# A hand-written order of all engines in the up projection of a convolutional feed-forward layer, with gated products on VectorE and sums of weights spread over the tiles

## The chip, the cores and the metric

The kernel runs on one core of a Trainium2 chip. Five engines run side by side, each with an instruction queue of its own, served in order, and they wait for each other with semaphores: TensorE (PE in the profile, its weight loads PEld), VectorE (DVE), ScalarE (ACT), GpSimd (POOL) and SyncE (SP), which here issues the transfers. The metric is the device time of one execution in microseconds, as the median of several runs. The result must agree with the reference in float32; matrix products therefore work with operands that are split in two.

## The reference

One transformer-like layer over 512 tokens of width 1024: a mixer of a state-space branch and a sparse attention, a feed-forward layer with a short convolution, and a gated embedding. The part that the change touches is the feed-forward layer:

```python
h = h + conv_ffn(rmsnorm(h, g_ffn[i]), w_up[i], conv_w[i], conv_b[i], w_down[i])

def conv_ffn(x, w_up, conv_w, conv_b, w_down):
    hid = x @ w_up                                   # 512 x 1024 @ 1024 x 5632
    hid = lax.conv_general_dilated(hid, conv_w[:, None, :], window_strides=(1,), padding=[(CONV_WIDTH - 1, 0)], ...) + conv_b
    a, b = jnp.split(hid, 2, axis=-1)
    return (jax.nn.gelu(a) * b) @ w_down             # 2816 x 1024
```

## The kernel before

**Split products.** Each float32 operand is held as a high part (ScalarE's `copy` into fp32r, L75) and a low part (the difference, `tt(lo, src, hi, SUB)`, L54). A product is three matmuls (`mm3`, L82 to L84): high by high, high by low, low by high. For the up projection these are `wh` with `n2h`, `wh` with `n2l` and `wl` with `n2h`, where `n2h` and `n2l` are the normalized activations.

**Tiles of the up projection.** The hidden width 2816 is cut in NF = 22 tiles of 128. Tile f has an a half (PSUM tile `ua`) and a b half (`ub`), each with a 1024 x 128 block of `w_up`, that is 8 blocks of contraction with 3 matmuls of 128 x 512 each: 48 matmuls for a tile. `wload` loads a raw block into one of three buffers `wr` (512 KB, L188), ScalarE copies the high part `wh`, and the low part `wl` is made by VectorE for the a half and by GpSimd for the b half; `wh` and `wl` have two buffers each. Tiles 0 and 1 are done in pieces, together with the end of the stage before; from f = 2 on all tiles are alike.

**Convolution and gate.** `convolved` takes each half from PSUM: ScalarE writes `cv` with one weight and the bias (L1495), VectorE adds the two delayed terms (`stt`, L63, 128 x 511 and 128 x 510). Then ScalarE does the Gelu of the a half (L1499). `Summed.add` makes the gated product in two pieces of 128 x 256 on GpSimd and, for the down projection, splits it (`ffa`, on ScalarE and VectorE) and forms sums of the pieces (`ffs`: S1 to S4) on VectorE. The down projection multiplies matrices in 2 x 2 blocks with seven products in place of eight, which is what all those sums are for. A hidden tile with odd number (e = 1) has three more of these steps than an even one.

**Sums of weights.** For the same reason sums of blocks of `w_down` are needed (`park`: two loads of 512 KB into tiles `b`, four additions of 128 x 512 on VectorE), and sums of blocks of `w_ple_gate` (`gate_parks`: four loads into `gb`, five sums, each split into `gph` on ScalarE and `gpl` on VectorE). They are made inside the up projection and written to DRAM (`bs`, `gs`) by `store_sums` and `leave`, and are loaded again later. `park_at` says at which tile each of the eleven blocks of `w_down` is done: two at f = 2, one at f = 3 and 8, one at each of 13 to 19. The gate sums lie at f = 2 to 12.

**What sets the order.** In the up projection no order is written out: a scheduler orders every engine's instructions by estimated times, with hints (`tc.issue_after(last(engine))`) that place the work on the sums of weights behind what its engine was given last. From the down projection on, TensorE, SP, ScalarE and VectorE run as written (`tc.manual_schedule`).

## Time and profile before

| | us |
|---|---|
| median of 3 runs | 791.77 (791.34 to 793.2) |
| the profiled execution | 793.93 |
| its span in the trace | 792.2 |
| TensorE / VectorE / ScalarE / GpSimd busy | 769.6 / 613.9 / 433.3 / 270.5 |
| up projection, f = 2 to 21 | 406.73 to 632.41 in the span |

The page of the profile gives busy times, and then the groups of instructions by line. A row of a timeline has the start, the duration, the engine, the line of the code, the operation, the tile written and the tiles read, and the size; in square brackets stands the idle time before it and what ended it. A row of waits has the waiting engine, tile and line, what it waited for, the sum of the waits, their number and the longest. Matmuls overlap in the pipeline, so the distance between two starts is the cost of one, not its duration.

### The profile page before, as it was taken

What the parts mean: (1) busy time and instruction counts of PE and PEld (TensorE: products, weight loads), DVE (VectorE), ACT (ScalarE), POOL (GpSimd) and SP (SyncE); (2) the same over time, 40 slices, a digit from 0 to 9 for tenths busy, and PEclk for the clock granted to TensorE, in tenths of its full rate; (3) what the DMA queues carried; (4) which work ended last, traced back from release to release, by engine and by line L of the source; (5) the groups of instructions that cost most, each with busy time, mean ns of one, the idle gap of its engine ahead of it and who ended that gap; (6) DMA issues with size and microseconds to landing.
All of it is one profiled execution on the core that took longest, in us unless ns stands there. A gap on an engine that the chain in (4) does not pass through costs nothing.

```text
span 792.2 us, 12336 instructions
## 1 busy us (share of the span) xinstructions
PE 769.6 (97%) x4362; PEld 645.7 (82%) x4362; DVE 613.9 (77%) x1152; ACT 433.3 (55%) x779; POOL 270.5 (34%) x303
## 2 busy tenths in 40 slices
PE   9999999999999999999999999999999999999993
PEld 7887878888888888888998887887777888888883
DVE  7987999766677739798696889987677587877586
ACT  6836655657777654435645454543434465745754
POOL 3577433136464534001125344432332310000125
PEclk9999999999999999999999999999999999999997
DMA  8944121424234136201097597567885365668752
GB/s 340 366 160 149 60 89 48 141 77 109 56 107 153 61 121 252 88 19 54 23 399 273 209 345 245 190 247 273 294 271 180 133 233 205 226 213 293 277 213 106
DMA packets 52077, 144.54 MB, mean 182 GB/s; under 512 B 6192, under 2 KB 8624, under 8 KB 52016
## 3 DMA queue, kind: packets, MB, share of 16 engines
q1 hardware_dynamic: 51440, 142.71, 51.5%
q10 hardware_dynamic: 576, 1.05, 0.4%
q8 instruction: 34, 0.56, 0.3%
q14 instruction: 27, 0.22, 0.1%
HBM read 112.28 MB, written 27.26 MB: 176 GB/s over the span
## 4 chain that ended last, share of the span: by engine, by line
PE 70%; DVE 15%; DMA 5%; issue 3%; POOL 3%; ACT 2%; SPq 1%; POOLq 0%; DVEq 0%; ACTq 0%
PE pj L82 6%; PE pj L83 5%; PE pj L84 5%; PE p L84 4%; PE p L82 4%; PE p L83 4%; DMA b<-in_w_down_dram 4%; DVE b L54 3%; DVE cv L63 2%; PE ua L84 2%; PE ua L83 2%; PE ua L82 2%; PE sps L1089 2%; PE ub L84 2%; PE ptp L1109 2%
## 5 line engine op out<-in xcount | busy, mean ns | idle before, releaser
L54 POOL TENSOR_TENSOR wl<-wr,wh 128x1024 fp32r<-128x1024 f32 x45 | 113.4, 2521 | 239.2 <-ACT wh L75 224.9
L75 ACT ACTIVATE wh<-wr 128x1024 fp32r<-128x1024 f32 x96 | 100.7, 1050 | 81.0 <-issue 24.5
L82 PE MATMUL pj<-n1h,wh 128*128 128x512 f32 x224 | 90.9, 406 | 0.4 <-DVE QT L54 0.4
L83 PE MATMUL pj<-n1l,wh 128*128 128x512 f32 x224 | 87.9, 392 | 0.0
L84 PE MATMUL pj<-n1h,wl 128*128 128x512 f32 x224 | 87.7, 392 | 0.0
L54 DVE TENSOR_TENSOR wl<-wr,wh 128x1024 fp32r<-128x1024 f32 (+1 forms) x51 | 64.3, 1261 | 22.5 <-ACT wh L75 21.8
L84 PE MATMUL ub<-n2h,wl 128*128 128x512 f32 (+1 forms) x168 | 65.3, 389 | 2.9 <-POOL wl L54 2.9
L84 PE MATMUL ua<-n2h,wl 128*128 128x512 f32 (+1 forms) x168 | 64.7, 385 | 1.5 <-DVE wl L54 1.5
L82 PE MATMUL ua<-n2h,wh 128*128 128x512 f32 (+1 forms) x168 | 64.8, 386 | 0.7 <-ACT wh L75 0.7
L83 PE MATMUL ua<-n2l,wh 128*128 128x512 f32 (+1 forms) x168 | 64.7, 385 | 0.0
L82 PE MATMUL ub<-n2h,wh 128*128 128x512 f32 (+1 forms) x168 | 64.6, 385 | 0.0
L83 PE MATMUL ub<-n2l,wh 128*128 128x512 f32 (+1 forms) x168 | 64.5, 384 | 0.0
L84 PEld LDWEIGHTS pj<-n1h,wl 128*128 128x128 f32 x224 | 42.1, 188 | 8.9
L82 PEld LDWEIGHTS pj<-n1h,wh 128*128 128x128 f32 x224 | 42.1, 188 | 8.4 <-DVE QT L54 0.9
L83 PEld LDWEIGHTS pj<-n1l,wh 128*128 128x128 f32 x224 | 42.2, 188 | 7.4 <-issue 0.2
L60 POOL TENSOR_SCALAR pr<-pr,su,gates 128x512 f32<-128x512 f32 (+2 forms) x64 | 38.7, 618 | 16.5 <-DVE su L1101 16.1
L54 POOL TENSOR_TENSOR cv<-cv 128x256 f32<-128x256 f32 x22 | 21.6, 983 | 61.1 <-DVE cv L63 47.2
L75 ACT ACTIVATE ph<-ptp 128x128 fp32r<-128x128 f32 (+1 forms) x64 | 27.9, 435 | 26.1 <-PE ptp L1109 26.0
L54 DVE TENSOR_TENSOR pl<-ptp,ph 128x128 fp32r<-128x128 f32 (+1 forms) x64 | 31.1, 486 | 14.3 <-ACT ph L75 13.3
L63 DVE SCALAR_TENSOR_TENSOR cv<-ub,cols,cv 128x511 f32<-128x511 f32 (+1 forms) x44 | 32.8, 744 | 12.0 <-ACT cv L1495 11.2
L84 PEld LDWEIGHTS ub<-n2h,wl 128*128 128x128 f32 x168 | 31.6, 188 | 11.5 <-POOL wl L54 5.5
L84 PEld LDWEIGHTS ua<-n2h,wl 128*128 128x128 f32 x168 | 31.6, 188 | 8.6 <-DVE wl L54 2.4
(509 smaller groups left out, 2108.8 us busy)
## 6 DMA issues: line engine op xcount, KB each, us to landing
wr<-in_w_up_dram SPq DMA_DIRECT2D x44, 512.0 KB, 4.6
wr<-in_w_in_dram SPq DMA_DIRECT2D x28, 512.0 KB, 3.9
b<-in_w_down_dram SPq DMA_DIRECT2D x22, 512.0 KB, 5.8
bs<-b SPq DMA_DIRECT2D x44, 256.0 KB, 2.5
ue<-bs SPq DMA_DIRECT2D x21, 512.0 KB, 4.5
wr<-in_w_down_dram SPq DMA_DIRECT2D x11, 512.0 KB, 4.9
gs<-gph SPq DMA_DIRECT2D x10, 512.0 KB, 2.6
gs<-gpl SPq DMA_DIRECT2D x10, 512.0 KB, 3.2
```

The costliest lines, as they stand in the source:

```text
L54: e.tensor_tensor(o, a, b, op=op)
L60: e.tensor_scalar(o, a, s1, s2, op0=op0, op1=op1)
L63: e.scalar_tensor_tensor(o, a, s, b, op0=op0, op1=op1)
L75: S.activation(o, a, AF.Copy)
L82: PE.matmul(ps, lh, rh, start=start, stop=False, skip_group_check=goes_on)
L83: PE.matmul(ps, lh, rl, start=False, stop=False, skip_group_check=goes_on)
L84: PE.matmul(ps, ll, rh, start=False, stop=stop, skip_group_check=goes_on)
L1089: PE.matmul(o, self.QQ[:, x, qt * P:(qt + 1) * P], KK[:, :, self.g, :w] if both else KK[:, self.br, self.g, :w], start=x == 0, stop=x == 1)
L1109: PE.transpose(ps[:, (qt - kt) * P:(qt - kt + 1) * P], self.pr[qt][:, kt * P:(kt + 1) * P], ident)
```

## The change

Nothing that is computed changes. From f = 2 on, all five queues are written out in one order of the program (`manual_schedule` over all engines):

- *TensorE.* In each half of a tile the 16 matmuls with `wh` come first (`up_half`), then the 8 with `wl` (`up_end`).
- *GpSimd* keeps the low part of the b half; the gated products (`times`) go to VectorE. Only the products of tiles 0 and 21 stay on GpSimd.
- *The gate of a tile is done one tile later*, with the convolution of its b half: `conv(f - 1, 1)` and `hidden(f - 1)` stand in tile f, `conv(f, 0)` and `gelu(f)` at its end. `Summed.add` is taken apart in `times`, `high`, `low` and `low2` for this.
- *Weights.* `up_high` and `up_low` make the parts of tile f + 1 at the end of tile f, apart from `up_low(f, 1, G)`, which stands in tile f.
- *Sums of weights* get new places (`down_at`, `half_at`, `gate_at`: the gate sums at f = 5 to 14; block 10 of `w_down` is done half at f = 8 and half at f = 12). Each is cut in a `first` part (`sums_a`) and a `second` part (`sums_z`, at the tile's end). Loads for `w_down` stand a tile ahead of their sums, and stores in the tile behind (`leave`), after that tile's loads.

```diff
-        def add(self, e, x, y):
-            tt(x[:, :HT], x[:, :HT], y[:, :HT], MUL, G)
-            tt(self.A22 if e else self.S1, x[:, HT:], y[:, HT:], MUL, G)
-            split(*self.A[e], x[:, :HT])
+        def times(self, e, x, y, v=V):
+            tt(x[:, :HT], x[:, :HT], y[:, :HT], MUL, v)
+            tt(self.A22 if e else self.S1, x[:, HT:], y[:, HT:], MUL, v)
+        def high(self, e, x):
+            copy(self.A[e][0], x[:, :HT])
+        def low(self, e, x):
+            tt(self.A[e][1], x[:, :HT], self.A[e][0], SUB)
             if e == 0:
                 tt(self.S3, self.S1, x[:, :HT], SUB)
                 return
             tt(x[:, HT:], self.A22, self.S3, SUB)
-            split(*self.S2, x[:, HT:])
+            copy(self.S2[0], x[:, HT:])
+            tt(self.S1, self.S1, self.A22, SUB)
+        def low2(self, x):
+            tt(self.S2[1], x[:, HT:], self.S2[0], SUB)
             tt(self.S4, x[:, :HT], x[:, HT:], SUB)
-            tt(self.S1, self.S1, self.A22, SUB)
+        def add(self, e, x, y):
+            self.times(e, x, y, G)
+            self.high(e, x)
+            self.low(e, x)
+            if e:
+                self.low2(x)
...
-        yield
-        hid[p_].add(f % 2, cv[:, 0], cv[:, 1])
...
+    steps = ((0, (1, 1), None), (1, (0, 0), (0, 1)), (3, (0, 1), (1, 1)), (2, (1, 1), (0, 0)), (4, (1, 0), (1, 1)))
+    down_at = {2: 0, 3: 1, 4: 2, 5: 3, 10: 9, **{15 + n: 4 + n for n in range(5)}}
+    half_at = {8: 0, 12: 1}
+    HALVES = NP - 1
...
+    def loads(f):
+        if f + 1 in down_at:
+            down_loads(down_at[f + 1])
+        if f == 7:
+            down_loads(HALVES)
+        for q, f0 in enumerate((2, 8)):
+            if f == f0:
+                gp[q].loads((1, 1), (0, 0))
+            if f == (5, 10)[q]:
+                gp[q].loads((0, 1), (1, 0))
...
+    def sums_a(f):
+        if half_at.get(f) == 0:
+            dp[HALVES].first()
+        if gate_at(f):
+            q, n = gate_at(f)
+            gp[q].first(*steps[n])
+        if f in down_at:
+            dp[down_at[f]].first()
+    def sums_z(f):
+        if gate_at(f):
+            gp[gate_at(f)[0]].second()
+        if f in down_at:
+            dp[down_at[f]].second()
+        if half_at.get(f) == 1:
+            dp[HALVES].second()
...
+    def up_half(f, ab):
+        hi, ps = uws[f, ab][0], ups[f][1][ab]
+        for k in range(KD):
+            PE.matmul(ps, hi[:, k], n2h[:, k], start=k == 0, stop=False)
+            PE.matmul(ps, hi[:, k], n2l[:, k], start=False, stop=False)
+    def up_end(f, ab):
+        lo, ps = uws.pop((f, ab))[1], ups[f][1][ab]
+        for k in range(KD):
+            PE.matmul(ps, lo[:, k], n2h[:, k], start=False, stop=k == KD - 1)
...
+    written = ExitStack()
+    written.enter_context(tc.manual_schedule(engines={mybir.EngineType.PE, mybir.EngineType.SP, mybir.EngineType.DVE,
+                                                      mybir.EngineType.Activation, mybir.EngineType.Pool}))
...
+    for f in range(2, NF):
+        up_raw(f + 1, 1)
+        loads(f)
+        up_raw(f + 2, 0)
         leave()
-        for c in range(NP):
-            if park_at[c] == f:
-                park(c)
-        if 2 <= f <= 12:
-            next(parks[f > 7], None)
-            if f == 7:
-                next(parks[1])
-        ups[f] = wab, [bank(either(), "ua"), bank("acc" if f == 1 else "s", "ub")]
-        if f == 1:
-            up(1, 0, 256)
-            up(0, 256, 512)
-            for _ in convolved(0):
-                pass
-            up(1, 256, 512)
-            for k_ in kept:
-                k_.done()
-        elif f < NF - 1:
-            up(f, 0, 512)
-        if f < NF - 1:
-            for _ in convolved(f):
-                pass
-        if f == NF - 2:
-            free[2].append(cvs[f % 2])
+        ups[f] = None, [bank(either(), "ua"), bank("s", "ub")]
+        up_half(f, 0)
+        conv(f - 1, 1)
+        up_low(f, 1, G)
+        h, e, x = hidden(f - 1)
+        h.times(e, x, cvt[f - 1][:, 1])
+        h.high(e, x)
+        up_end(f, 0)
+        sums_a(f)
+        up_half(f, 1)
+        h.low(e, x)
+        up_end(f, 1)
+        conv(f, 0)
+        if f + 1 < NF:
+            up_high(f + 1, 0)
+        else:
+            hid[NR].split_sums(0)
+            wd[NR] = w_of(NR)
+        gelu(f)
+        if e:
+            h.low2(x)
+        if f + 1 < NF:
+            up_low(f + 1, 0)
+            up_high(f + 1, 1)
+        sums_z(f)
+    free[2].append(cvs[NF % 2])
+    written.close()
```

The new `conv` and `gelu` hold what `convolved` held; the classes `Park` and `GatePark` hold the four additions and the five split sums of `park` and `gate_parks`, cut in two parts each.

On VectorE, at the sums of w_down in the tiles behind the gate sums, the order before was this (`cv` is the convolution, `b` the block of `w_down`, `ffa` and `ffs` belong to the gated product):

```order
L54 TENSOR_TENSOR wl<-wr,wh 128x1024
L63 SCALAR_TENSOR_TENSOR cv<-ua,cols,cv 128x511
L63 SCALAR_TENSOR_TENSOR cv<-ua,cols,cv 128x510
L54 TENSOR_TENSOR b_6026<-b_6027,b_6026 128x512
L54 TENSOR_TENSOR b_6027<-b_6027 128x512
L54 TENSOR_TENSOR b_6027<-b_6027,b_6026 128x512
L54 TENSOR_TENSOR b_6026<-b_6027,b_6026 128x512
L63 SCALAR_TENSOR_TENSOR cv<-ub,cols,cv 128x511
L63 SCALAR_TENSOR_TENSOR cv<-ub,cols,cv 128x510
L54 TENSOR_TENSOR ffa<-cv,ffa 128x256
L54 TENSOR_TENSOR cv<-ffs_5906 128x256
```

and the order of the changed kernel at the first of its tiles of this kind, f = 15, is this, from the second step of the convolution of `ub` on:

```order
L63 SCALAR_TENSOR_TENSOR cv<-ub,cols,cv 128x510
L54 TENSOR_TENSOR cv<-cv 128x256
L54 TENSOR_TENSOR ffs_6097<-cv 128x256
L54 TENSOR_TENSOR b_6022<-b_6023,b_6022 128x512
L54 TENSOR_TENSOR b_6023<-b_6023 128x512
L54 TENSOR_TENSOR ffa<-cv,ffa 128x256
L54 TENSOR_TENSOR ffs_6097<-ffs_6097,cv 128x256
L63 SCALAR_TENSOR_TENSOR cv<-ua,cols,cv 128x511
L63 SCALAR_TENSOR_TENSOR cv<-ua,cols,cv 128x510
L54 TENSOR_TENSOR wl<-wr,wh 128x1024
L54 TENSOR_TENSOR b_6023<-b_6023,b_6022 128x512
L54 TENSOR_TENSOR b_6022<-b_6023,b_6022 128x512
```

The convolution of `ub` now opens the tile, the two products (`cv<-cv` and the `ffs` behind it) follow on VectorE, and the four sums lie two behind the products and two behind the low part `wl`, where before all four lay between the two convolutions.

On ScalarE, in a tile with a gate block and an odd hidden tile, the order before was this (L1495 is the convolution's first term, L1499 the Gelu):

```order
L75 ACTIVATE wh<-wr 128x1024
L75 ACTIVATE gph<-gb 128x1024
L1495 ACTIVATE cv<-ub,cols 128x512
L1499 ACTIVATE cv<-cv 128x512
L75 ACTIVATE wh<-wr 128x1024
L1495 ACTIVATE cv<-ua,cols 128x512
L75 ACTIVATE ffa<-cv 128x256
L75 ACTIVATE ffs_5733<-cv 128x256
```

and it is now this (L1511 and L1516 are the same two operations):

```order
L1511 ACTIVATE cv<-ub,cols 128x512
L75 ACTIVATE ffa<-cv 128x256
L75 ACTIVATE gph<-gb 128x1024
L75 ACTIVATE ffs_5915<-cv 128x256
L1511 ACTIVATE cv<-ua,cols 128x512
L75 ACTIVATE wh<-wr 128x1024
L1516 ACTIVATE cv<-cv 128x512
L75 ACTIVATE wh<-wr 128x1024
```

The copies for the gated product (`ffa`, `ffs`) and for the gate block (`gph`) now stand ahead of the convolution of `ua`, and the two high parts `wh` behind it, on either side of the Gelu.

On SP, around two blocks of `w_down` (`b` loads, `bs` stores of sums), the queue before held this:

```order
L188 DMA b_6026<-in_w_down_dram 128x1024
L188 DMA b_6027<-in_w_down_dram 128x1024
L188 DMA wr<-in_w_up_dram 128x1024
L1527 DMA bs_6111<-b_6026 128x512
L1527 DMA bs_6111<-b_6027 128x512 x2
L1527 DMA bs_6111<-b_6026 128x512
L188 DMA b_6116<-in_w_down_dram 128x1024
L188 DMA b_6117<-in_w_down_dram 128x1024
```

and it now holds this:

```order
L188 DMA wr<-in_w_up_dram 128x1024
L188 DMA b_6199<-in_w_down_dram 128x1024
L188 DMA b_6200<-in_w_down_dram 128x1024
L188 DMA wr<-in_w_up_dram 128x1024
L1548 DMA bs_6205<-b_6022 128x512
L1548 DMA bs_6205<-b_6023 128x512 x2
L1548 DMA bs_6205<-b_6022 128x512
L188 DMA wr<-in_w_up_dram 128x1024
```

The stores of one block now stand behind the load of the next block and behind the tile's loads of `w_up`; before, they stood ahead of that load.

More of the change, by code (lines that the diff above doesn't have):

```diff
@@ L1503, in hybrid_kernel, with hidden, __init__, first @@
+    def hidden(f):
+        return hid[f // 2], f % 2, cvt[f][:, 0]
     sums = {}
     parked = []
-    def park(c):
-        x, y = Slot("b1", 2), Slot("b2", 2)
-        with tc.issue_after(last(mybir.EngineType.SP)):
-            for i, t in enumerate((x, y)):
-                wraw("w_down", D, 2 * c * P, i * 512, 2, 512, raw=t.parts())
-        a, b = x.parts(), y.parts()
-        with tc.issue_after(last(mybir.EngineType.DVE)):
+    class Park:
+        def __init__(self, c):
+            self.c, self.t = c, (Slot("b1", 2), Slot("b2", 2))
+            self.a, self.b = (t.parts() for t in self.t)
+            for i, t in enumerate((self.a, self.b)):
+                wraw("w_down", D, 2 * c * P, i * 512, 2, 512, raw=t)
+        def first(self):
+            a, b = self.a, self.b
@@ L1514, in park, with second @@
             tt(a[:, 0], b[:, 0], a[:, 0], ADD)
             tt(b[:, 0], b[:, 1], b[:, 0], ADD)
+        def second(self):
+            a, b = self.a, self.b
             tt(b[:, 1], b[:, 1], a[:, 0], ADD)
             tt(a[:, 1], b[:, 1], a[:, 1], ADD)
-        parked.append((c, x, y))
-    def store_sums():
-        while parked:
-            c, x, y = parked.pop()
-            a, b = x.parts(), y.parts()
-            sums[c] = pud.tile([4, P, 512], F32, name=f"bs{c}")
-            with tc.issue_after(last(mybir.EngineType.SP)):
-                for n, t in enumerate((a[:, 0], b[:, 1], b[:, 0], a[:, 1])):
-                    nc.sync.dma_start(sums[c][n], t)
-            x.done()
-            y.done()
+            leaving.append(self.stored)
@@ new lines, in hybrid_kernel, with __init__, loads, first @@
+    class GatePark:
+        def __init__(self, q):
+            self.q, self.blocks = q, {}
+        def loads(self, *where):
+            for k, i in where:
+                self.blocks[k, i] = s_ = Slot("gb", 2)
+                wraw("w_ple_gate", D, 2 * (2 * k + self.q) * P, i * 512, 2, 512, raw=s_.parts())
+        def first(self, n, o, x):
+            self.n, self.o = n, self.blocks[o]
+            self.hl = [Slot(f"gp{y}", 2, F32R) for y in "hl"]
+            if x:
+                tt(self.o.t, self.o.t, self.blocks[x].t, ADD)
+            copy(self.hl[0].t, self.o.t)
+        def second(self):
+            n, hl = self.n, self.hl
+            tt(hl[1].t, self.o.t, hl[0].t, SUB)
+            leaving.append(lambda: self.stored(n, hl))
@@ new lines, in hybrid_kernel @@
+    for ab in range(2):
+        keep = [kept[2 * ab + x].parts(KD) for x in range(2)]
+        wab.append(wload("w_up", 2 * DFF, 0, ab * DFF + P, KD, P, (V, G)[ab], keep=keep))
+    ups[1] = wab, [bank(either(), "ua"), bank("acc", "ub")]
+    up(1, 0, 256)
+    up(0, 256, 512)
+    for ab in range(2):
+        conv(0, ab)
+    gelu(0)
+    hid[0].add(0, cvt[0][:, 0], cvt[0][:, 1])
+    up(1, 256, 512)
+    for k_ in kept:
+        k_.done()
+    for f, ab in ((2, 0), (2, 1), (3, 0)):
+        up_raw(f, ab)
@@ L1646, in hybrid_kernel @@
         sums_b(NR)
-        next(last_conv)
+        conv(NF - 1, 1)
         wd[NR + 1] = w_of(NR + 1)
```

119 lines of the change are left out of this document (57 added, 62 removed).

## The prediction

> **What bounds the kernel now.** I read four views in this order: the page's busy times, then the up projection alone in a window, then the TensorE waits, then the chain of waits. The page says that TensorE is nearly always busy:
>
> ```profile
> PE 769.6 (97%) x4362; PEld 645.7 (82%) x4362; DVE 613.9 (77%) x1152; ACT 433.3 (55%) x779; POOL 270.5 (34%) x303
> ```
>
> An order of the other engines can therefore win only what TensorE loses to waiting. The twenty tiles f = 2 to 21 of the up projection begin at the first row below and end where the down projection's first product begins:
>
> ```profile
> 406.73 0.40 PE L82 MATMUL ua<-n2h,wh 128*128 128x512 f32 x1
> ...
> 417.63 0.39 PE L82 MATMUL ua<-n2h,wh 128*128 128x512 f32 x1
> ...
> 428.51 0.39 PE L82 MATMUL ua<-n2h,wh 128*128 128x512 f32 x1
> ...
> 632.41 0.39 PE L82 MATMUL p<-wh,ffa 128*128 128x512 f32 x1
> ...
> 406.73:632.41 225.68, 220.58 (x962) 179.37 (x961) 176.28 (x229) 99.90 (x140) 85.86 (x59) 1.00 0.70 248
> ```
>
> An undisturbed tile of 48 products takes 428.51 - 417.63 = 10.88 us (0.227 us from start to start), so twenty would take 217.6 us. The stage takes 225.68 us at a granted clock of 1.00. **8.1 us is lost**, and that is all that this change can win here. The waits of TensorE in that window name who was late:
>
> ```profile
> PE ub L84 <- POOL wl L54: 2.9, 4, 1.0
> PE ua L84 <- DVE wl L54: 1.5, 2, 1.0
> PE ua L82 <- ACT wh L75: 0.7, 2, 0.4
> ```
>
> That is 5.1 us of plain idling; the rest of the 8.1 us is the pipeline's refill, since a stopped stream costs more than its idle gap:
>
> ```profile
> 556.87 0.39 PE L83 MATMUL ub<-n2l,wh 128*128 128x512 f32 x1
> 558.23 0.50 PE L84 MATMUL ub<-n2h,wl 128*128 128x512 f32 x1 [0.98 <-POOL wl L54]
> 558.57 0.40 PE L82 MATMUL ub<-n2h,wh 128*128 128x512 f32 x1
> ```
>
> Here 0.98 us of idling costs 1.36 + 0.34 - 2 x 0.227 = 1.25 us. The chain shows why the low part was late. VectorE stood in its queue in front of a load, and everything behind it moved:
>
> ```profile
> 534.91 6.04 DMA b<-in_w_down_dram
> ...
> 541.07 0.70 DVE b L54
> 541.80 2.78 DVE b L54
> ...
> 546.72 0.76 DVE cv L63
> ...
> 547.61 0.74 POOL cv L54
> 548.37 0.43 ACT ffa L75
> ```
>
> The sums of w_down wait for their load, the convolution waits behind the sums, GpSimd's gated product behind the convolution, ScalarE's copy ffa behind the product, and in ScalarE's queue the next wh stands behind ffa. TensorE has no reserve against this, because it wants the low part two products after the high part of the same tile.
>
> **The change, part by part.** Matmuls are neither added nor removed. In each half the 16 products with wh come first and the 8 with wl last. With 0.227 us each, measured from a tile's start, wh of the a half is wanted at 0, wl(a) at 3.6, wh(b) at 5.4, wl(b) at 9.1. Before, wl was wanted 0.45 us after wh in both halves. This edit costs nothing in itself: the same 48 products, each with its own weight load.
>
> VectorE gets two gated products per tile. The prices come from a stretch in which VectorE ran without a pause; the distance of two starts is the price:
>
> ```profile
> 504.88 1.22 DVE L54 TENSOR_TENSOR gb<-gb 128x1024 f32<-128x1024 f32 x1
> 506.01 0.74 DVE L63 SCALAR_TENSOR_TENSOR cv<-ua,cols,cv 128x511 f32<-128x511 f32 x1
> 506.67 0.42 DVE L54 TENSOR_TENSOR ffa<-cv,ffa 128x256 fp32r<-128x256 f32 x1
> 507.00 2.62 DVE L54 TENSOR_TENSOR ffs<-cv 128x256 f32<-128x256 f32 x1
> 509.55 0.41 DVE L54 TENSOR_TENSOR ffs<-cv,ffs 128x256 fp32r<-128x256 f32 x1
> 509.89 0.73 DVE L63 SCALAR_TENSOR_TENSOR cv<-ua,cols,cv 128x510 f32<-128x510 f32 x1
> 510.55 1.21 DVE L54 TENSOR_TENSOR gpl<-gb,gph 128x1024 fp32r<-128x1024 f32 x1
> 511.68 1.52 DVE L63 SCALAR_TENSOR_TENSOR cv<-ub,cols,cv 128x511 f32<-128x511 f32 x2
> 513.12 1.21 DVE L54 TENSOR_TENSOR wl<-wr,wh 128x1024 fp32r<-128x1024 f32 x1
> ...
> 588.72 1.41 DVE L54 TENSOR_TENSOR b<-b,b 128x512 f32<-128x512 f32 x2
> ...
> 506.63 2.71 POOL L54 TENSOR_TENSOR wl<-wr,wh 128x1024 fp32r<-128x1024 f32 x1 [2.47 <-ACT wh L75]
> ```
>
> So 0.33 us for 128x256, 1.13 for 128x1024, 1.44 for two dependent convolution steps, 0.7 for one 128x512 sum. VectorE's work per tile is then 2 x 1.44 (convolution) + 2 x 0.33 (products) + 1.13 (wl) + 2 x 0.33 for an even hidden tile or 5 x 0.33 for an odd one: 5.3 or 6.3 us. Four sums of w_down add 2.8, a gate block 2.26, half of block ten 1.4. The fullest tiles are f = 10 (odd hidden tile 9, a gate block without an add, four sums): 6.3 + 1.13 + 2.8 = 10.2; and f = 8 and 12: 6.3 + 2.26 + 1.4 = 10.0. **Every tile fits in 10.88 us**, if nothing holds VectorE up.
>
> What could hold it up is the row of 2.62 us: a 0.42 us step that ran beside GpSimd's wl and ended only after it (506.63 + 2.71 = 509.34). The convolution step at 506.01, which reads PSUM and one SBUF tile, ran through. The Trainium skill says this too (SBUF — State Buffer, "Who interferes with whom"): a VectorE instruction with two SBUF inputs and a GpSimd instruction that reads SBUF shut each other out for a whole instruction. By that rule alone products moved to VectorE are two more instructions to be shut out; the trace agrees, with 2.62 against 0.42 us. Whether they meet is a question of place. In the changed order GpSimd has only wl(b), and may start when the last product of the previous tile frees the buffer, 0.16 us into the tile (0.39 - 0.227). It ends at about 2.6. In that time VectorE does the two convolution steps of the b half, from 1.0 (0.16 plus ScalarE's 0.76 us below) to 2.5. The lock costs about 0.1 us then; it costs up to 2.4 where VectorE is behind and still in its sums. I take 0.1, with 2.4 as the other end.
>
> ```profile
> L75 ACT ACTIVATE wh<-wr 128x1024 fp32r<-128x1024 f32 x39 | 41.1, 1054 | 27.1 <-PE ua L83 11.7 <-issue 7.7 <-PE ub L83 7.4
> L1495 ACT ACTIVATE cv<-ub,cols 128x512 f32<-128x512 f32 x20 | 15.2, 762 | 2.1 <-PE ub L84 2.1
> L1499 ACT ACTIVATE cv<-cv 128x512 f32<-128x512 f32 x20 | 12.6, 629 | 35.8 <-DVE cv L63 35.6
> L75 ACT ACTIVATE ffa<-cv 128x256 fp32r<-128x256 f32 x20 | 8.3, 417 | 49.2 <-POOL cv L54 49.2
> ```
>
> Now the tile f = 8 by these rows, in the written order. VectorE: convolution b to 2.5, products to 3.2, two sums of block ten to 4.6, gate add to 5.7, three low steps to 6.7. ScalarE copies ffa behind the first product, the gate block from 5.7 to 6.8, S2 to 7.2, and only then starts on ua (finished since 5.6): to 7.9, then wh(a) of the next tile to 9.0. VectorE: convolution a 7.9 to 9.4, low steps to 10.0, wl(a) to 11.2. TensorE wants that wh at 10.9 and that wl at 14.5: **1.9 and 3.3 us of margin in the worst tile**. ScalarE's Gelu ends at 10.0, wh(b) at 11.1 (wanted at 16.3); GpSimd's wl(b) at 13.5 (wanted at 20.0). In a tile without sums convolution a starts at 6.4 and wl(a) ends at 9 to 9.6, so 5 us are free. The waits that go are all of the kind "a low part came late", and what is late next, wh(a), has 2 us.
>
> VectorE's new waits are in-order ones: behind the convolution of ua stand its low steps and wl(a), for which TensorE waits only at 14.5. SP's queue is written too. The w_down loads go out a tile earlier than their sums, so the 6.04 us of the chain lie beside a whole tile. Stores stand behind the loads of w_up on SP and wait there for sums that ended in the tile before. A load of w_up goes out when a raw buffer is free, for wr(b) when wl(a) of the tile before is done, by 0.3 in the worst tile, and ScalarE wants it at 10.0:
>
> ```profile
> wr<-in_w_up_dram SPq DMA_DIRECT2D x35, 512.0 KB, 4.8
> b<-in_w_down_dram SPq DMA_DIRECT2D x18, 512.0 KB, 5.5
> ```
>
> So some 5 us are free here as well. At the start nothing new waits (the high and low parts of tile 2 are made during tile 1 as before); at the end wh and wl of the first w_down block are made inside tile 21, by about 9.6 of 10.88, and the uh copy waits for n2h in both kernels.
>
> **Sum.** 225.7 us become 20 x 10.89 = 217.8, a gain of 7.9; I keep 0.1 for single pauses: **-7.8**. The profiled execution took 793.93 us (span 792.2), so it would become 786.1. That execution lies 2.16 above the median of the three runs shown, 791.77 (791.34 to 793.2); off that median the forecast is **784.0 us**. Behind the stage TensorE's longest wait is this one, so an earlier start there is kept to the end:
>
> ```profile
> PE px L82 <- ACT pq L1976: 0.5, 1, 0.5
> ```
>
> **The rivals.**
> - *Not all of it (786 to 789).* VectorE gets behind in full tiles, its sums meet GpSimd's wl, and 2.4 us go each time. With the lock in every tile, f = 8, 10 and 12 need 12.4, 12.6 and 12.4 us, 1.5 to 1.7 too many; f = 7, 9 and 11 (5.3 + 2.3 + 2.4 = 10.0) give back 0.9 each, and f = 2 to 6 add up to about 1.6 before. VectorE would then stand 3.7 us behind at the end of f = 12, about all of the margin of 3.3 to 5. If four tiles stop as long as at 556.87, 4 x 1.25 = 5.0 come back: 789.0; with two, 786.5. By the rule on the shared port in the Trainium skill (SBUF — State Buffer, "Who interferes with whom") this is the outcome if the two engines meet in each tile. What speaks against it is the place worked out above: VectorE reaches the products as wl(b) ends.
> - *Given back (within 0.3%, about 791).* The down projection opens with little reserve:
>
> ```profile
> 633.70 1.23 DVE L54 TENSOR_TENSOR ul<-wr,uh 128x1024 fp32r<-128x1024 f32 x1 [2.87 <-ACT uh L75]
> ...
> 635.36 0.39 PE L83 MATMUL p<-ul,ffs 128*128 128x512 f32 x1
> ```
>
> ul ends at 634.93 and is used at 635.36, 0.4 us later. If the work that VectorE carries over from tile 21, or the loads behind it, come later by as much as the stage is shorter, the gain is only moved there. Against it: uh and ul hang on the end of n2h's use, which comes earlier with the stage, and they keep their place in the queues; the loads that they need were stored long before.
> - *Slower, by transfers (about 805).* The written queue puts 3.15 MB into nearly every tile (two w_up blocks and two pairs of loads or groups of stores, 1.05 MB each time). At the stage's 248 GB/s (last number of the window's row) that is 12.7 us, 1.8 more than a tile. If transfers cannot run faster than this, sixteen such tiles fall 29 us behind; the lighter ones and the 5 us of reserve give 7 back and the forecast's gain 8: 14 us slower. It decides once a w_up block lands later than about 12 us after issue, against a median of 4.8. Against it stands a stretch of the same stage, with the same kinds of transfer, in which they ran at 399 GB/s, where 3.15 MB take 7.9 us:
>
> ```profile
> 400.00:410.00 10.00, 10.00 (x73) 9.43 (x72) 9.83 (x15) 4.06 (x6) 3.17 (x3) 1.00 1.04 399
> ```
>
> **How the numbers follow.** Forecast 0.76 (783.2 to 785), not all of it 0.14, given back 0.06, slower 0.04. A measurement of this kernel tells about 0.3%, 2.4 us, from no change. The forecast and nearly all of the second case are beyond that: faster 0.88; the third, and the rest of the second: same 0.07; slower 0.05, with a little for queues that I have not seen. The range takes the forecast's own and the mild half of the second case: 783.0 to 786.8.
>
> **What would show it.** Right: no TensorE wait for wl or wh in the stage, twenty tiles of 10.9 us, GpSimd's wl of 2.4 us beside the b convolution, products of 0.4 us behind it, no VectorE wait for a w_down load. Wrong: products or sums of 2 us and more, wl(a) ending later than 3.6 us into the next tile, w_up blocks that land after 10 us, or waits for uh, ul or wl right behind the stage.

## The result, and the profile after

| | before | after |
|---|---|---|
| median of 4 runs, us | 791.87 (791.34 to 793.2) | 786.34 (785.81 to 786.37) |
| ratio, 95% interval | | 0.9926 (0.991 to 0.9942) |
| the profiled execution, us | 793.93 | 786.37 |
| its span, us | 792.2 | 784.6 |
| tiles f = 2 to 21, us | 225.68 | 217.84 |

The kernel is 0.74% faster: 5.5 us between the medians, 7.6 between the two profiled executions. TensorE is now busy for all but 2% of the span. One execution of the unchanged kernel, of 1102.08 us at a granted clock of 0.654, is a slow one and is left out of every median and ratio here. The page has this, and below it the transfers (the last number is the median time from issue to landing, over the whole kernel):

```profile
PE 767.0 (98%) x4362; PEld 646.7 (82%) x4362; DVE 611.0 (78%) x1192; ACT 437.0 (56%) x779; POOL 233.3 (30%) x263
...
wr<-in_w_up_dram SPq DMA_DIRECT2D x44, 512.0 KB, 4.4
...
b<-in_w_down_dram SPq DMA_DIRECT2D x22, 512.0 KB, 6.0
```

The window over the twenty tiles (its length; busy times of PE, PEld, DVE, ACT and POOL; granted clock, DMA share, GB/s):

```profile
406.74:624.58 217.84, 217.84 (x962) 180.16 (x961) 177.23 (x273) 103.80 (x141) 49.89 (x19) 1.00 0.74 255
```

TensorE is busy in all of it. The view of waits names none of TensorE in these tiles, where it named 5.1 us before, and no wait of VectorE for a load of w_down. After the stage the longest one is what it was:

```profile
PE px L82 <- ACT pq L2086: 0.5, 1, 0.5
```

The timeline has the stage's first and last rows, and between them the places where it came nearest to a stop:

```profile
406.74 0.40 PE L1664 MATMUL ua<-n2h,wh 128*128 128x512 f32 x1
...
504.70 3.49 DVE L54 TENSOR_TENSOR b<-b,b 128x512 f32<-128x512 f32 x2
...
504.99 2.65 POOL L54 TENSOR_TENSOR wl<-wr,wh 128x1024 fp32r<-128x1024 f32 x1 [8.47 <-PE ub L1670]
...
526.75 3.24 POOL L54 TENSOR_TENSOR wl<-wr,wh 128x1024 fp32r<-128x1024 f32 x1 [7.33 <-PE ub L1670]
...
527.66 3.61 DVE L54 TENSOR_TENSOR b<-b,b 128x512 f32<-128x512 f32 x2
...
536.31 1.05 ACT L75 ACTIVATE wh<-wr 128x1024 fp32r<-128x1024 f32 x1
...
537.41 0.50 PE L1664 MATMUL ua<-n2h,wh 128*128 128x512 f32 x1
...
624.58 0.39 PE L82 MATMUL p<-wh,ffa 128*128 128x512 f32 x1
```

Two additions of w_down blocks take 1.41 us elsewhere; at 504.70 and 527.66, beside GpSimd's wl(b), they took 3.49 and 3.61. VectorE came out of the second 2.2 us late, and wh of tile 14 ended at 537.36, 0.05 us before its first product. That product was already held up a little: tiles 13 and 14 took 10.96 and 11.01 us, all others 10.88 (tile 2: 10.91), so 0.2 us went there.

In the kernel before, such meetings were frequent, and one stands in the chain that the prediction reads. These are its rows in the timeline of that kernel:

```profile
541.07 0.69 DVE L54 TENSOR_TENSOR b<-b,b 128x512 f32<-128x512 f32 x1 [1.38 <-DMA b<-in_w_down_dram]
541.50 2.52 POOL L54 TENSOR_TENSOR wl<-wr,wh 128x1024 fp32r<-128x1024 f32 x1 [5.22 <-ACT wh L75]
541.80 2.77 DVE L54 TENSOR_TENSOR b<-b 128x512 f32<-128x512 f32 x1
```

The wait for the load cost VectorE 1.38 us; the next sum, beside GpSimd's low part, took 2.77 us in place of 0.69, which is 2.1 us more. Over the stage of the kernel before, twelve of VectorE's steps took more than 1 us longer than the same step elsewhere, each beside a wl of GpSimd, 22 us in all and the same in all three of its profiles; VectorE's waits for w_down loads come to 5.2 us. In the changed kernel there are two such steps, 4.2 us in all.

So TensorE's waits for low parts are gone, as forecast, and the gain between profiled executions (7.84 us in the stage) is the forecast 7.9. Between medians it is 5.5. The experiments ask where the difference is, which of the three parts is worth what, and how near the new order is to failing.

### The profile page after: what moved, and what is told of

Read it like the earlier page. It is cut to its first block, busy times and chain, and to the rows that moved or that the text cites. A ratio compares the mean times of both kernels' runs of the same rounds, so it can differ in the third digit from the quotient of the medians.

```text
span 784.6 us, 12279 instructions
## 1 busy us (share of the span) xinstructions
PE 767.0 (98%) x4362; PEld 646.7 (82%) x4362; DVE 611.0 (78%) x1192; ACT 437.0 (56%) x779; POOL 233.3 (30%) x263
## 4 chain that ended last, share of the span: by engine, by line
PE 87%; DVE 6%; DMA 2%; issue 2%; ACT 1%; POOL 1%; SPq 0%; POOLq 0%; DVEq 0%; ACTq 0%
PE pj L82 6%; PE pj L83 6%; PE pj L84 6%; PE ua L1664 5%; PE ua L1665 5%; PE ub L1664 5%; PE ub L1670 5%; PE ua L1670 5%; PE ub L1665 5%; PE p L84 4%; PE p L82 4%; PE p L83 4%; PE sps L1089 2%; PE ptp L1109 2%; PE br L82 2%; PE br L84 2%
## 5 line engine op out<-in xcount | busy, mean ns | idle before, releaser
L54 DVE TENSOR_TENSOR wl<-wr,wh 128x1024 fp32r<-128x1024 f32 (+1 forms) x51 | 62.0, 1216 | 18.6 <-ACT wh L75 18.6
L1664 PE MATMUL ua<-n2h,wh 128*128 128x512 f32 x160 | 62.4, 390 | 0.0
L1665 PE MATMUL ua<-n2l,wh 128*128 128x512 f32 x160 | 62.3, 389 | 0.0
L1664 PE MATMUL ub<-n2h,wh 128*128 128x512 f32 x160 | 62.3, 389 | 0.0
L1665 PE MATMUL ub<-n2l,wh 128*128 128x512 f32 x160 | 62.2, 389 | 0.0
L63 DVE SCALAR_TENSOR_TENSOR cv<-ua,cols,cv 128x511 f32<-128x511 f32 (+1 forms) x44 | 32.9, 749 | 23.5 <-ACT cv L1511 22.7
L1670 PE MATMUL ub<-n2h,wl 128*128 128x512 f32 x160 | 39.5, 389 | 0.0
L1670 PE MATMUL ua<-n2h,wl 128*128 128x512 f32 x160 | 39.5, 389 | 0.0
L75 ACT ACTIVATE ffa<-cv 128x256 fp32r<-128x256 f32 x22 | 9.2, 418 | 53.0 <-DVE cv L54 46.5
L1100 ACT ACTIVATE pr<-pr,nb 128x512 f32<-128x512 f32 (+2 forms) x64 | 35.5, 558 | 3.0 <-DVE nb L1098 2.9
```

The lines of the kernel that those rows point to most:

```text
L54: e.tensor_tensor(o, a, b, op=op)
L63: e.scalar_tensor_tensor(o, a, s, b, op0=op0, op1=op1)
L75: S.activation(o, a, AF.Copy)
L1100: S.activation(pp, pp, AF.Exp, bias=nb, scale=-1.0, accum_out=su)
L1664: PE.matmul(ps, hi[:, k], n2h[:, k], start=k == 0, stop=False)
L1665: PE.matmul(ps, hi[:, k], n2l[:, k], start=False, stop=False)
```

## The experiments

"Stage" is the time from the first product of tile 2 to the first of the down projection, "rest" the profiled execution's time less its stage. The interval is for the ratio to the kernel before on the same chip. The runs come from three chips, on which the kernel before had medians of 792.17, 791.37 and 791.57 us, and the rest differs between kernels by up to 1.6 us (567.84 to 569.44). Small differences between medians from different chips are therefore better read from the stages.

| kernel | median, us | ratio (95%) | stage, us | rest, us |
|---|---|---|---|---|
| before, again | 792.51 | 1.0002 (0.9991 to 1.0013) | 224.31 | 568.54 |
| before, third profile | 793.17, one run | | 224.63 | 568.54 |
| before, low parts last | 792.41 | 1.0007 (0.9997 to 1.0016) | 224.84 | 568.44 |
| after, products mixed | 789.09 | 0.9965 (0.9954 to 0.9976) | 220.82 | 567.84 |
| after, gate on GpSimd | 788.04 | 0.9949 (0.9934 to 0.9964) | 219.14 | 568.92 |
| after, both undone | 790.63 | 0.9987 (0.9977 to 0.9997) | 222.03 | 568.53 |
| after, block ten moved | 786.40 | 0.9939 (0.9924 to 0.9953) | 217.62 | 568.68 |
| gate on GpSimd, block ten moved | 786.48 | 0.9939 (0.9922 to 0.9955) | 217.63 | 569.34 |
| after, wl(a) made twice | 822.46 | 1.0393 (1.0376 to 1.041) | 254.73 | 568.44 |
| after, wl(b) on VectorE | 786.97 | 0.9945 (0.993 to 0.996) | 217.89 | 569.44 |
| after, loads in the sums' tile | 803.27 | 1.015 (1.0133 to 1.0167) | 235.94 | 568.09 |
| the same, wl(b) on VectorE | 801.28 | 1.0126 (1.0111 to 1.0141) | 232.73 | 569.08 |

### How much a usual execution of the kernel before loses

No edit: the kernel before, twice more.

> The kernel before, unchanged. In its first profiled execution the twenty tiles took 225.68 us and everything else 793.93 - 225.68 = 568.25 us; in the changed kernel they took 217.84 and everything else 786.37 - 217.84 = 568.53. Theory A (the stops themselves differ from execution to execution): everything else is 568.3 +-0.4 again, and an execution of 791.4 to 792 us has a stage of 223.0 to 223.8, so that the loss that can be won is 5.4 to 6.2 us and not 8.1. Theory B (the profiled execution was longer by something that lies outside the stage, as the forecast took it when it went down from 786.1 by 2.16): the stage is 225.7 +-0.3 in every profile, and everything else is about 566.1 in an execution of 791.8.

> The kernel before once more, for a third pair of stage and time. The first two: stage 225.68 and 224.31, time 793.93 and 792.85, everything else 568.25 and 568.54. Theory A (executions differ by their stops in the stage): stage = time - 568.4 within 0.5 us. Theory B: a stage that doesn't go with the time.

The stage of the second execution, by the first and the last row of the timeline:

```profile
407.03 0.40 PE L82 MATMUL ua<-n2h,wh 128*128 128x512 f32 x1
...
631.34 0.39 PE L82 MATMUL p<-wh,ffa 128*128 128x512 f32 x1
```

And of the third, with its waits in the view of waits:

```profile
406.98 0.40 PE L82 MATMUL ua<-n2h,wh 128*128 128x512 f32 x1
...
631.61 0.39 PE L82 MATMUL p<-wh,ffa 128*128 128x512 f32 x1
```

```profile
PE ub L84 <- POOL wl L54: 2.5, 3, 1.1
PE ua L82 <- ACT wh L75: 1.2, 1, 1.2
PE ua L84 <- DVE wl L54: 1.0, 1, 1.0
```

Three executions of one program: stage 225.68, 224.31 and 224.63, rest 568.25, 568.54 and 568.54. The stops are of the same kinds but not of the same number or length (four for GpSimd's low part in the first, three in the others). Theory A holds in all three and B in none: what makes one execution longer than another lies in the stage. For a median of 791.87 this gives a stage of 791.87 - 568.44 = 223.4 and a loss of 223.4 - 217.6 = 5.8 us. Only profiled executions show their stage, so for the median one this is inferred; that four runs of a kernel without stops spread by 0.7 us or less (785.81 to 786.37, 786.28 to 786.63, 786.64 to 787.33) and the kernel before by 4.4 in 26 runs (789.79 to 794.21) and by 1.9 in four points the same way. Stops need not differ from run to run, though: ten runs of the kernel with both parts undone, in which four tiles take longer than 10.88 us, spread by 0.8 us.

### One part alone: low parts last

```diff
+            if f >= 2:
+                for k in range(KD):
+                    PE.matmul(pss[ab], hi[:, k], n2h[:, k], start=k == 0, stop=False)
+                    PE.matmul(pss[ab], hi[:, k], n2l[:, k], start=False, stop=False)
+                for k in range(KD):
+                    PE.matmul(pss[ab], lo[:, k], n2h[:, k], start=False, stop=k == KD - 1)
+                continue
             for k in range(KD):
                 mm3(pss[ab][:, t0:t1_], hi[:, k], lo[:, k], n2h[:, k, t0:t1_], n2l[:, k, t0:t1_],
...
```

> The kernel before with one part of the change alone: in tiles 2 to 21 the 16 products with wh come first and the 8 with wl last; the scheduler still orders the other engines, and it moves them too. Theory A (the low part was late by about 1 us against a need 0.45 us after the high part, so 3.1 us of reserve remove nearly every stop): stage 217.8 to 219.5, time 786.3 to 788.0. Theory B (the order of the engines is what delays the low part, by more than the reserve, and the scheduler spends the reserve again): TensorE still waits for wl or wh by 3 us and more, time 789.5 to 792.

792.41 us, no gain. TensorE's waits in the stage now read:

```profile
PE ua L1311 <- ACT wh L75: 2.7, 4, 1.0
PE ub L1311 <- ACT wh L75: 1.7, 2, 1.4
PE ua L1314 <- DVE wl L54: 0.7, 1, 0.7
```

5.1 us again, but for the high part. The longest one, in ScalarE's timeline (line 1502 writes cv, 1506 is Gelu):

```profile
539.27 0.76 ACT L1502 ACTIVATE cv<-ua,cols 128x512 f32<-128x512 f32 x1
543.61 0.63 ACT L1506 ACTIVATE cv<-cv 128x512 f32<-128x512 f32 x1 [3.57 <-DVE cv L63]
544.14 1.04 ACT L75 ACTIVATE wh<-wr 128x1024 fp32r<-128x1024 f32 x1
```

The high part stands in ScalarE's queue behind a Gelu that waited 3.57 us for VectorE's convolution. Reserve for the low part doesn't help a high part that is late. In this kernel VectorE still has 14 steps that take over 1 us longer than elsewhere beside GpSimd's wl, 26 us in all. Theory B: without the written order this part is worth nothing.

### Parts undone in the written order

Products mixed:

```diff
             PE.matmul(ps, hi[:, k], n2l[:, k], start=False, stop=False)
+            PE.matmul(ps, uws[f, ab][1][:, k], n2h[:, k], start=False, stop=k == KD - 1)
 
     def up_end(f, ab):
-        lo, ps = uws.pop((f, ab))[1], ups[f][1][ab]
-        for k in range(KD):
-            PE.matmul(ps, lo[:, k], n2h[:, k], start=False, stop=k == KD - 1)
+        uws.pop((f, ab))
```

> The changed kernel with the products of each half mixed again (wh, wh, wl for each k), all written orders kept. By the hand table of the prediction wl(b) is then wanted at 5.9 us and ends at 2.6, and wl(a) is wanted 0.45 us into the tile: it ends 9 to 9.6 us into the tile before in tiles without sums, and 0.3 us into the tile in the fullest. Theory A (the written order alone suffices but for the fullest tiles): no stop in tiles with wl(a) ending below 10.9, stage 217.8 to 219, time 786.3 to 787.5. Theory B (low parts last are what removes the stops): VectorE's wl(a) is late in many of the ten tiles with four sums or a gate block, each stop about 1 us: stage 221 to 226, time 790 to 794.

Gate on GpSimd:

```diff
-        h.times(e, x, cvt[f - 1][:, 1])
+        h.times(e, x, cvt[f - 1][:, 1], G)
```

> The changed kernel with the two gated products of each tile back on GpSimd, behind wl(b) in its queue; VectorE has 0.66 us less per tile. GpSimd then ends the products at about 2.6 + 2 x 0.75 = 4.1 us into the tile, and ScalarE's ffa, VectorE's low steps follow 1 us later than in the changed kernel. Theory A (TensorE has its reserve from the place of wl, not from the engine of the products): no stop, 786.3 +-0.4. Theory B (the products on VectorE are a needed part): GpSimd and the engines behind it fall behind in the tiles with sums, stops of about 1 us in several of them, 788 to 791.

Both:

> The changed kernel with two of its parts undone: products of a half mixed again (alone: 789.1) and gated products on GpSimd (alone: 788.0). What is left is the written order, the loads a tile ahead and the spread sums. Theory A (each part removes its own stops, and they add): 786.3 + 2.75 + 1.7 = 790.8, between 789.8 and 791.5. Theory B (without the two parts VectorE falls behind for good and meets wl(b)): above 794.

With the products mixed (789.09) the waits are

```profile
PE ua L1666 <- DVE wl L54: 2.3, 3, 0.9
```

three stops, at tiles 9, 12 and 14. In the changed kernel wl(a) ends 0.4, 0.5 and 1.7 us into these; in most tiles it ends 0.7 us or more ahead. It ends late for tiles 13 and 15 too (0.2 and 1.3 us), but here these come right behind a stop, which gives VectorE that time back. That is between the two theories: the written order alone suffices for seventeen tiles, and behind the fullest ones wl last is needed. With the gate on GpSimd (788.04) there is one stop, at tile 14, where theory A had none and theory B several:

```profile
PE ua L1664 <- ACT wh L75: 1.2, 1, 1.2
```

With both undone 790.63, against a sum of 786.34 + 2.75 + 1.70 = 790.8: the two add up, as theory A says. The stages say the same: 217.84 + 2.98 + 1.30 = 222.1 against 222.03. What is left, the order, the early loads and the spread sums, is worth 0.9 us by itself (790.63 against 791.57 of the kernel before on the same chip; ratio 0.9987, 0.9977 to 0.9997), low parts last by itself nothing, and all together 5.5.

The written order by itself does bring VectorE's long steps beside wl from twelve to two (4.3 us in all), and yet it wins only 0.9 us. Being on time and having reserve each win little without the other. How much of the 5.5 us is due to the removed meetings was not isolated: no run removes them alone from the kernel before.

### Where the reserve is: tile 14

The last two sums of block ten go from the end of tile 12 into tile 11:

```diff
-    half_at = {8: 0, 12: 1}
+    half_at = {8: 0, 11: 1}
...
         if f in down_at:
             dp[down_at[f]].first()
+        if half_at.get(f) == 1:
+            dp[HALVES].second()
...
             dp[down_at[f]].second()
-        if half_at.get(f) == 1:
-            dp[HALVES].second()
```

> The changed kernel with the last two sums of block ten not at the end of tile 12 but behind the gate block's add in tile 11. In the changed kernel they began at 527.66, beside GpSimd's wl(b) (526.75 to 529.99), and took 3.61 us where two such sums take 1.41; after that wh of tile 14 ended at 537.36, when TensorE began on it at 537.41: no reserve at all, and the tiles 13 and 14 took 10.96 and 11.01. Theory A (VectorE and GpSimd shut each other out, and this pair alone eats the reserve of tile 14): two sums in tile 11 take 1.4 us, wh of tile 14 ends 1.5 to 2.5 us ahead of its tile, all tiles from 3 on 10.88 to 10.92; time 786.1 to 786.4, which can't be told from the changed kernel. Theory B (tile 12 and 13 are too full in themselves): wh of tile 14 still ends within 0.5 us of its use.

> Products on GpSimd (the kernel of 788.04 us, with one stop of 1.22 us where tile 14 waits for its wh) and the last two sums of block ten in tile 11 as well. Theory A (the stop came from the sums that met GpSimd's wl(b) in tile 13, plus the 1 us that GpSimd's products add): the stop is gone, stage 217.8 to 218.2, time 786.4 to 787.0. Theory B (GpSimd's products make tile 13 too long in any case): TensorE still waits about 1 us for wh of tile 14 or a neighbour, 787.7 to 788.3.

In the first of the two the timeline has the moved sums, the wh of tile 14, and that tile's first product at 537.26:

```profile
511.41 1.41 DVE L54 TENSOR_TENSOR b<-b,b 128x512 f32<-128x512 f32 x2
...
533.46 1.05 ACT L75 ACTIVATE wh<-wr 128x1024 fp32r<-128x1024 f32 x1
...
537.26 0.39 PE L1664 MATMUL ua<-n2h,wh 128*128 128x512 f32 x1
```

The sums take 1.41 us in place of 3.61, wh ends 2.75 us ahead of its tile (a little more than the 1.5 to 2.5 expected), and the stage is 217.62, the twenty undisturbed tiles. In time that can't be told from the changed kernel. In the kernel with the gate on GpSimd it can: the stop is gone and the time falls from 788.04 to 786.48. Theory A holds in both (the second stage, 217.63, is even below the 217.8 expected). So products on VectorE were worth 1.7 us only through this one tight place; with it removed, they are worth 0.1, and the stages of the two kernels are equal.

### An overload of 1.13 us per tile

VectorE makes wl(a) twice in a row:

```diff
-    def up_low(f, ab, e=V):
+    def up_low(f, ab, e=V, twice=False):
...
+        if twice:
+            tt(t, uraws[f, ab], uws[f, ab][0], SUB, e)
         tt(t, uraws.pop((f, ab)), uws[f, ab][0], SUB, e)
...
-            up_low(f + 1, 0)
+            up_low(f + 1, 0, twice=True)
```

> The changed kernel with VectorE's wl(a) of the next tile made twice in a row in each tile (the same values again): 1.13 us more for VectorE per tile, and with it wl(a) and all that follows on VectorE 1.13 us later. The reserve of wh in the changed kernel is 3.1 to 3.5 us in most tiles, 2.0 at tile 9, 1.3 at 12, 1.2 at 15 and 0.05 at 14. Theory A (reserve by tile, no spreading): one stop, at tile 14, of 1.0 to 1.3 us, as in the kernel with the products on GpSimd; stage 218.9 to 219.4, time 787.4 to 788.0. Theory B (an engine that is behind meets GpSimd's wl each time and loses 2.2 us more): stops at 9, 12, 14 and 15 of 1 us and more each, stage above 221, time 789.5 to 792.

822.46 us: 36 us slower, far beyond both theories, though in the direction of B. What the waits of TensorE show:

```profile
PE ua L1672 <- DVE wl L54: 16.6, 9, 1.9
PE ua L1666 <- ACT wh L75: 9.1, 7, 2.2
```

The timeline has, first, VectorE and GpSimd in one tile, and then two of the stops that follow from such tiles:

```profile
466.83 4.63 DVE L54 TENSOR_TENSOR wl<-wr,wh 128x1024 fp32r<-128x1024 f32 x2
...
468.00 2.38 POOL L54 TENSOR_TENSOR wl<-wr,wh 128x1024 fp32r<-128x1024 f32 x1 [11.17 <-ACT wh L75]
...
524.33 2.11 PE L1672 MATMUL ua<-n2h,wl 128*128 128x512 f32 x8 [1.91 <-DVE wl L54]
...
603.41 2.52 PE L1672 MATMUL ua<-n2h,wl 128*128 128x512 f32 x8 [1.92 <-DVE wl L54]
```

The second wl(a) began about when GpSimd's wl(b) did and came out behind it: 4.63 us for two that take 2.4; TensorE then stands 1.9 us. In each of the tiles 3 to 21 one of VectorE's steps meets wl(b) and takes 2.1 to 2.2 us longer than elsewhere, 41 us in all. Over the stage, grouped by line (the last number before the bar of idle time is the mean in ns):

```profile
L54 DVE TENSOR_TENSOR wl<-wr,wh 128x1024 fp32r<-128x1024 f32 x39 | 67.0, 1717 | 0.6
...
L54 DVE TENSOR_TENSOR gpl<-gb,gph 128x1024 fp32r<-128x1024 f32 x10 | 23.1, 2312 | 0.0
```

To tell this from plain overload, the same 1.13 us was added in another way: wl(b) on VectorE and nothing on GpSimd.

```diff
-        up_low(f, 1, G)
+        up_low(f, 1)
```

> The changed kernel with the low part of the b half made on VectorE at the same place of the order, so that GpSimd does nothing in the stage. VectorE's load grows by the same 1.13 us per tile as where wl(a) was made twice (822.5 us). Theory A (that kernel was slow because VectorE, once behind, meets GpSimd's wl(b) with an operation of two SBUF inputs and stands 2.2 to 3.4 us, tile after tile): without GpSimd's wl no operation of VectorE takes longer than its price, the fullest tiles need 11.1 to 11.3 us for one tile each, stops of at most 1.5 us in all; stage 217.7 to 220, time 786.3 to 788.6. Theory B (1.13 us more per tile is itself too much for VectorE): stage 250 and more, time about 820.

786.97 us. The same groups of this kernel, and its stage as a window:

```profile
L54 DVE TENSOR_TENSOR wl<-wr,wh 128x1024 fp32r<-128x1024 f32 x40 | 48.7, 1218 | 0.0
...
L54 DVE TENSOR_TENSOR gpl<-gb,gph 128x1024 fp32r<-128x1024 f32 x10 | 12.2, 1220 | 0.0
```

```profile
407.14:625.03 217.89, 217.89 (x962) 180.11 (x961) 190.61 (x293) 102.11 (x141) 0.00 (x0) 1.00 0.75 256
```

Same operations, 1218 and 1220 ns in place of 1717 and 2312, and the view of waits names none of TensorE. The stage is 0.05 us longer than the changed kernel's; the rest of the 0.6 us between the medians lies outside it. Theory A holds: it was not the amount of work. (The added 1.13 us stands at the tile's start here and at its end there; this place was not varied by itself.) An engine that is late meets the other's long instruction, which makes it later by 2 us and more, so that it meets it again in the next tile. It does not recover, because such a tile needs more than 10.88 us. The windows of the overloaded kernel (the stage, and three pieces around one stop) have a second cost:

```profile
406.66:661.39 254.73, 229.07 (x963) 183.35 (x961) 233.29 (x292) 100.27 (x141) 50.06 (x19) 0.97 0.64 218
...
603.00:606.00 3.00, 2.59 (x9) 2.15 (x10) 2.93 (x5) 0.00 (x0) 0.00 (x0) 0.82 0.54 156
606.00:608.50 2.50, 2.50 (x7) 1.94 (x7) 2.43 (x7) 1.82 (x3) 0.00 (x0) 0.53 1.04 352
608.50:612.00 3.50, 3.50 (x17) 2.87 (x17) 3.43 (x6) 1.75 (x3) 0.00 (x0) 1.00 0.98 291
```

Of the 36.9 us by which the stage is longer, 25.7 are the waits above; in the other 11.2 TensorE counts as busy (229.07 against 217.84). Four stretches of 3.4 us at half the clock cost about 1.7 us each, 6.8 in all; the remaining 4.4 fit the refill of the pipeline behind sixteen stops, at the 0.27 us each that the prediction's row at 558.23 gives (1.25 less 0.98).

### Loads in the tile of their sums

```diff
-        if f + 1 in down_at:
-            down_loads(down_at[f + 1])
-        if f == 7:
+        if f in down_at and f > 2:
+            down_loads(down_at[f])
+        if f == 8:
             down_loads(HALVES)
```

> The changed kernel with the two loads of w_down for each block issued in the tile of its sums, not the tile before (the first block excepted). They take 6.0 us to land, so the first two sums can begin about 5 us into the tile and not 3.2: VectorE stands about 2 us in each of ten tiles. Theory A (the written order has the reserve for it): no stop but perhaps at tile 9 or 11, time 786.3 to 787.6. Theory B (VectorE standing before a load is what stopped TensorE in the kernel before, whatever the order): TensorE waits for wh or wl in five or more tiles, time 789 to 793.

> The loads of w_down in the tile of their sums (803.3 us, stage 235.9), with wl(b) on VectorE as well. Theory A (the wait for the load, some 2 us in a tile, was not what cost 18 us; it made VectorE late enough to meet GpSimd's wl(b)): VectorE is 1.13 us fuller, yet the stage falls to 218 to 223, time 786.5 to 791.5. Theory B (the waits for loads themselves are the cost): with more work on VectorE the time is 803 us or more.

803.27 and, with GpSimd out of it, still 801.28. The first is beyond both theories, the second 1.7 us below theory B's bound and 10 above theory A's. VectorE's meetings with wl(b), ten of over 1 us in the first kernel (21.6 us in all) and none in the second, are thus worth only 2 us here (3.2 in the stage), and A's explanation falls. The timeline of the second kernel (VectorE, and SP's queue) shows what VectorE waits for instead:

```profile
440.91 1.22 DVE L54 TENSOR_TENSOR wl<-wr,wh 128x1024 fp32r<-128x1024 f32 x1
...
442.15 0.33 SPq L188 DMA_DIRECT2D wr<-in_w_up_dram  x1
442.53 0.91 SPq L188 DMA_DIRECT2D b<-in_w_down_dram  x2
...
449.09 0.69 DVE L54 TENSOR_TENSOR b<-b,b 128x512 f32<-128x512 f32 x1 [2.39 <-DMA b<-in_w_down_dram]
...
452.54 1.22 DVE L54 TENSOR_TENSOR wl<-wr,wh 128x1024 fp32r<-128x1024 f32 x1
```

A ring. wl(a) ends at 442.13 and frees a raw buffer; SP, which stood before it, issues the w_up load at 442.15 and behind it the two w_down loads; VectorE waits for these until 449.09; behind the sums come the convolution and the next wl(a), which ends at 453.76. Once round is 453.76 - 442.13 = 11.6 us, more than a tile's 10.88, so in a row of such tiles VectorE is later each time, and the next load with it: wl(a) ends 0.0, 0.4, 2.4 and 3.0 us into tiles 3, 4, 5 and 6. With a gate block and an odd hidden tile in it, as in tiles 8 and 10, one round is enough for a stop. Tiles 6, 8, 10, 16 and 17 took 12.6 to 13.5 us. That the wait of 2.4 us is only a fifth of the ring is why a budget by tile missed it. With the loads a tile ahead the ring has two tiles, 21.8 us, and room. Of all that was undone here this costs most: 803.27 - 786.34 = 17 us. That the ring is the cause is read from this timeline and the code; it was not tried whether the loads could go ahead of the w_up load in the queue of the same tile.

## Why the prediction was right, and where it was not

- **The loss and its end.** 8.1 us lost in the profiled execution, a stage of 217.8 to come, the gain kept behind it: measured 217.84, span 7.6 us shorter, the wait px unchanged at 0.5. Right as far as TensorE goes: no low part comes late any more.
- **The mis-sized term is "That execution lies 2.16 above the median of the three runs shown ... off that median the forecast is 784.0 us".** This took the 2.16 us for something outside the stage that the changed kernel would have as well. The runs put it inside: the rest is 568.25 to 568.54 in all three profiles of the kernel before, so the 2.16 us were part of the 8.1 that the change removes, and the step counted them twice. From the median the loss is 5.8 us and the measured gain 5.5. The sum had already produced the right time one sentence earlier, 786.1 for an execution without stops, against 786.34 measured. The measured time lies outside the forecast's own 783.2 to 785 and inside the first rival's 786 to 789, though TensorE doesn't stop as that rival says. The range held it (783.0 to 786.8) only because its upper end reached into that rival, which is luck.
- **Why the low parts were late** is only half of the story in the prediction. It names the wait for the load. In the very chain that it shows, the row of 2.78 us is a sum of 0.7 beside GpSimd's wl, and that costs more than the wait (2.1 against 1.38 us).
- **The prices** (0.33 us a product or low step, 1.13 a wl, 1.44 a convolution, 0.7 a sum) and "Every tile fits in 10.88 us" held but for 0.2 us in tiles 13 and 14. That a convolution step runs through beside GpSimd's wl rested on an overlap of 0.12 us (506.63 to 506.75); it holds: in the changed kernel the steps beside wl(b) take 0.74 to 0.75 us in each tile.
- **The margins.** For f = 8 the hand table was right: the next wh ended 2.1 us ahead (1.9 forecast) and wl(a) 0.4 us into tile 9 (0.3 forecast). But f = 8 was not the worst tile. That was f = 13, whose wh for tile 14 had 0.05 us. The step that failed is "The lock costs about 0.1 us then": it cost 2.1 and 2.2 us at 504.70 and 527.66. The table ends with wl(a), at 11.2 in a tile of 10.88, and leaves out what stands behind it in VectorE's queue: the low part gpl in each gate tile, and in tiles 10 and 12 two sums more. These run into the next tile, where GpSimd's wl(b) is. The first rival's mechanism was at work, twice, and happened to be covered; "products or sums of 2 us and more", one of the prediction's own signs of being wrong, did show.
- **First rival (not all of it).** It came to 0.2 us at tile 14 and no more. With 1.13 us more per tile the mechanism decides, and its price is not the 2.5 to 5 us that the rival gave but 36, since being late repeats itself.
- **Given back** did not happen: no wait for uh, ul or wl behind the stage. **Slower by transfers** neither: a w_up block lands after 4.4 us (4.8 before) at 255 GB/s over the stage. (The window of 399 GB/s that the prediction holds against this rival lies mostly before the stage, which begins at 406.73; a window inside it, 406.73 to 416.73, has 386 GB/s, so the argument stands.) Here the queue's order, not its volume, was what could have gone wrong, and the ring of the last two experiments is that case.
- **The parts.** Low parts last was costed at nothing and was taken to give reserve. It does, 2.75 us' worth, but only in the written order. The gate on VectorE is worth 1.7 as things stand, and 0.1 with block ten moved.

By what the traces leave open, the stage of an unprofiled execution is inferred and not seen, and why the stops of the kernel before fall differently from run to run was not looked into. By order alone nothing is left to win in this stage: 217.62 to 217.89 us is what 960 products take at 0.227 us each.

## What to carry to other kernels

In this kernel a profiled execution's distance from the median was part of what the stops make, not a constant to subtract: take the time without stops as the forecast, and profile the kernel before more than once to see what varies. A step that takes several times its usual length is a cause of its own: look at what the other engines run beside it before blaming the wait ahead of it. Where two engines shut each other out and one runs long instructions, place the other's work by start times, not by the sum of its load: the same 1.13 us cost 0.6 us with GpSimd idle and 36 with GpSimd's low part in each tile. And look for rings (buffer freed, queue, load, sum, buffer freed): one that is longer than the period accumulates, however small the wait in it seems.

## What the hardware showed that was not expected

A stop of under 2 us was enough to lower TensorE's granted clock. In the overloaded kernel TensorE stood 1.92 us until 603.41 (row above). In the window from 606.00 to 608.50 the granted clock is 0.53, and the products start 0.43 us apart and not 0.227; from 608.50 on it is 1.00 again. The stage has three more such stretches, each of 3.4 us:

```profile
471.80:475.20 3.40, 3.40 (x9) 2.64 (x9) 3.33 (x6) 0.42 (x1) 0.00 (x0) 0.50 0.77 264
499.10:502.50 3.40, 3.40 (x10) 2.62 (x9) 3.33 (x6) 0.42 (x1) 0.00 (x0) 0.50 0.81 282
652.70:656.10 3.40, 3.40 (x9) 2.64 (x9) 2.59 (x6) 0.51 (x2) 0.00 (x0) 0.50 0.76 254
```

The Trainium skill (TensorE: Matmul & The Clock Gate, "What's actually happening") gives an idle window of about 3.4 us for this. Here the idle time was shorter, and the stop of 1.91 us until 524.33 was followed by eight products in 2.11 us where the other's eight took 2.52. The starts of the four stretches tell the two apart. With 604.9 for the one shown above, they lie 27.3, 105.8 and 47.8 us apart, which is 8, 31 and 14 times 3.413. On the grid of 3.413 us through them, the four stops of 1.87 to 1.92 us that lie inside one interval (until 471.52, 498.62, 603.41 and 652.41) were followed by an interval at half the clock, and the five of 1.89 to 2.21 us that fall across a border (until 445.04, 465.68, 524.33, 551.43 and 578.54) were not. A stop of 1.56 us inside one interval was not either (until 545.60). The two kernels with the loads in the sums' tile have one such stretch each, behind 1.88 and 2.43 us of idle time in one interval, and none behind 1.56. So in these runs the limit lies between 1.56 and 1.87 us of idle time within one interval, and where a stop falls in the interval decides as much as its length.

Two-input steps of VectorE and GpSimd's wl delay each other in both directions: wl(b), alone 2.4 us, took 2.65 and 3.24 us in the rows at 504.99 and 526.75. The Trainium skill (SBUF — State Buffer, "Who interferes with whom") states that the one which starts first holds the port for its whole instruction; the traces agree, with 3.61 against 1.41 us for the pair of sums.
